# Regrouping an expert's whole-array products, splitting one weight unit elsewhere, and holding one GpSimd product

## The chip, the cores and the metric

The kernel runs on 1 core of one Trainium2 chip. The metric is the device time of one execution in microseconds (us), as the median of the runs. The engines are TensorE (PE), VectorE (DVE), ScalarE (ACT), GpSimd (POOL) and SyncE (SP), whose queue starts the weight transfers.

## What is computed

An activation of 256 x 1024 passes two blocks in float32. The first has a mixer (stick-breaking attention beside a gated recurrence) and a mixture of 16 experts; the second has an ffn, a sparse-attention mixer and another ffn. Cut to what the change touches:

```python
def hgrn2_chunk_scan(q, k, log_f, v):          # gated recurrence, 8 heads of 64
    ...
        scores = jnp.einsum('bhtk,bhsk,bhtsk->bhts', qc, kc, decay)
        o = (jnp.einsum('bhts,bhsv->bhtv', scores, vc)
             + jnp.einsum('bhtk,bhkv->bhtv', qc * jnp.exp(cum), state))
...
def hier_moe(h, w_rg, b_rg, w_re, b_re, w_gate, w_up, w_down):
    ...
    for e in range(N_EXPERTS):                 # 16 experts, D_EXPERT = 512
        a = jax.nn.silu(t @ w_gate[e]) * (t @ w_up[e])
        y = y + combine[:, e:e + 1] * (a @ w_down[e]).astype(f32)
...
def swiglu(h, w_in, w_out):                    # both ffns, D_FF = 2816
    ...
    return (jax.nn.silu(gate) * up) @ w_out
```

Each token goes to two experts of one group of four, so the kernel gathers the tokens of an expert into 64 columns, works on these, and scatters the results back with a product.

## The kernel before, in words

The stages follow each other, and their spans in the profiled execution are: first mixer 0 to 236 us, experts (`moe`) 236 to 450, first `ffn` to 650, second mixer (`mixer2`) to 766, last `ffn` to the end. All weights pass once through SBUF: `Stream.load` puts units of 1 MB on SP's queue (L107), each into a slot that the users of an earlier unit gave back. The order in which a weight unit is posted is thus tied to the work that frees its slot.

Most weights are split into a high part, copied by ScalarE (L353 in `split_next`), and a low part, a subtraction by VectorE (L365, function `low`; its engine can be given). Three products are then summed: high by high, high by low, low by high. `split_next` posts the next load behind the low part. `unit` takes a split unit, splits the next one, and runs what stands in `pend`.

**Recurrence** (`hgrn`, L835 to 958) is one of the generators whose steps are laid between the projections of the first mixer. It goes through levels; in each, VectorE and GpSimd make scaled copies of keys and queries (L875, L883, L886, L888), TensorE multiplies them, and VectorE merges the scores (L900). The last level has the product of L903 instead. Afterwards two products `o = ih * dg` on GpSimd (L926) need nothing from the levels; VectorE adds TensorE's result `hpo` to each (L928). In this stage a scheduler of the language orders most of the work.

**Experts** (`moe`, from L963) are in an order written by hand. The loop at L1248 does for expert e: the first half of gate and up of expert e + 1 (`gate_up(e + 1, 0)`, L1193: 16 products, which use the array as 128*64), then `act(e)` (four transposes of the stored gate/up results into `pst`, L1205; silu on ScalarE, L318; the product `at` on VectorE, L1208) and `spread(e)` (two products `pso` from one-hot rows, L1215; VectorE takes from them `sc`, L1217, and `ws`, L1219). Then comes `gate_up(e + 1, 1)`, which ends with two ScalarE copies of the accumulated bank `gu` to `gs` (L1199); `scatter(e - 1)` (four whole-array products into `Y`, L1246); in three of the experts `gather` for the next group (L1129); and `down(e)` (16 products `dn`, 128*64, L1231, evacuated by ScalarE at L1238 and VectorE at L1240). `gu`, `pst`, `pso` and `dn` take turns in four PSUM banks.

**First ffn** (`ffn`, L1417): for each of 22 hidden tiles q, VectorE takes the sums from PSUM to `sg` (L1450). The function `later`, run within the next unit, has the silu (ScalarE), the product with the second half (VectorE, L1454) and the split into `ah` and `al` (L386, L387). Output units follow for pairs of tiles (L473 to L490). After the last one, `then` adds PSUM to `x` (L1486), multiplies by the norm gain to `y` (L1490), and TensorE transposes `y` (L1379) for the second mixer, whose first product is L1607. The weights of that first product are split after output unit NFT//2 - 2, with the low part on GpSimd.

Of the kernel before, what the change touches and what calls it, by code (L numbers as in the profile page):

```python
# [10 lines left out]
F32 = mybir.dt.float32  # L11
# [4 lines left out]
OP = mybir.AluOpType  # L16
# [6 lines left out]
NFT = FF // 128  # L23
E = 16
# [244 lines left out]
class K:  # L269
# [565 lines left out]
    def hgrn(self):  # L835
        nc, P = self.nc, self.P
        t4 = lambda n, **k: P.tile([128, 4, 256], F32, name=n, tag="t4", bufs=T4)
        sg, qh = self.sgf, self.qh
# [30 lines left out]
        for l in range(8):  # L869
            h = 1 << l  # L870
            nb = 256 // (2 * h)
            v = lambda x: x.rearrange("p f (b w i) -> p (f b) w i", w=2, i=h)
            if h > 1:
                self.act(1, v(kz)[:, :, 0], v(suf)[:, :, 0], AF.Exp)
                nc.vector.tensor_tensor(out=v(kz)[:, :, 0], in0=v(kz)[:, :, 0], in1=v(kk)[:, :, 0], op=OP.mult)  # L875
            else:
                nc.vector.tensor_copy(v(kz)[:, :, 0], v(kk)[:, :, 0])
            self.act(1, v(kz)[:, :, 1], v(pre)[:, :, 1], AF.Exp)
            if l < 7:
                w = lambda x: x.rearrange("p f (t b w i) -> p (f t) b w i", t=2, w=2, i=h)[:, :, :, 1]  # L880
                for g in range(2):
                    r = slice(g * 64, g * 64 + 64)
                    nc.vector.tensor_tensor(out=qq[r, :, g].rearrange("p a (b i) -> p a b i", i=h),  # L883
                                            in0=w(kz)[r], in1=w(qh)[r], op=OP.mult)
                B = [128, 4 * nb, h]
                nc.gpsimd.tensor_tensor(out=v(suf)[:, :, 0], in0=v(suf)[:, :, 0],  # L886
                                        in1=v(pre)[:, :, 1, h - 1:h].to_broadcast(B), op=OP.add)
                nc.gpsimd.tensor_tensor(out=v(pre)[:, :, 1], in0=v(pre)[:, :, 1],  # L888
                                        in1=v(pre)[:, :, 0, h - 1:h].to_broadcast(B), op=OP.add)
                yield 0, W_HG  # L890
                pss = [self.ps.tile([128, 4, 2, 64], F32, name=f"hs{t}", tag="s") for t in range(2)]
                for t in range(2):
                    for f in range(4):
                        nc.tensor.matmul(pss[t][:, f].rearrange("p g c -> p (g c)"), kz[:, f, t * 128:t * 128 + 128],
                                         qq[:, 2 * f + t].rearrange("p g c -> p (g c)"), start=True, stop=True)
                yield 1750, 0
                mk = self.c1[:, A_HM + l * 64:A_HM + l * 64 + 64].bitcast(I32).rearrange("p (b i) -> p b i", i=h)
                for t in range(2):
                    ac = acc[:, :, t].rearrange("p a (b w i) -> p a b w i", w=2, i=h)[:, :, :, 1]
                    nc.vector.copy_predicated(ac, mk[:, None].to_broadcast([128, 8, 64 // h, h]),  # L900
                                              pss[t].rearrange("p f g (b i) -> p (f g) b i", i=h))
            else:
                nc.vector.tensor_tensor(out=v(kz)[:, :, 1], in0=v(kz)[:, :, 1], in1=v(qh)[:, :, 1], op=OP.mult)  # L903
                yield 0, W_HG

                pss = [self.ps.tile([128, 4, 128], F32, name=f"hs{g}", tag="s") for g in range(2)]
                for f in range(4):
                    for g in range(2):
                        r = slice(g * 64, g * 64 + 64)
                        nc.tensor.matmul(pss[g][:, f], kz[r, f, :128], kz[r, f, 128:], start=True, stop=True)  # L910
                yield 1750, 0
                cross = t4("cross").rearrange("p a (b c) -> p (a b) c", b=2)
                for g in range(2):
                    nc.scalar.copy(cross.rearrange("p (f g) c -> p f g c", g=2)[:, :, g], pss[g])
            yield 0, 300
# [4 lines left out]
        for t in range(2):  # L920
            po = self.ps.tile([128, 8, 64], F32, name="hpo", tag="s")
            for hd in range(8):
                if t == 1:
                    nc.tensor.matmul(po[:, hd], cross[:, hd], ih[:, 0, hd], start=True, stop=False)
                nc.tensor.matmul(po[:, hd], acc[:, hd, t], ih[:, t, hd], start=t == 0, stop=True)
            nc.gpsimd.tensor_tensor(out=o[:, t], in0=ih[:, t],  # L926
                                    in1=dg[:, t, :, None].to_broadcast([128, 8, 64]), op=OP.mult)
            nc.vector.tensor_tensor(out=o[:, t], in0=po, in1=o[:, t], op=OP.add)  # L928
            yield 1700 * (1 + t), 300
        self.st.add(P, "b8", 3, U_FFN1 - 8)  # L930
# [32 lines left out]
    def moe(self, x, po):  # L963
# [3 lines left out]
        with tc.manual_schedule():  # L967
# [216 lines left out]
            def gate_up(e, u):  # L1184
                c = slice((e % 4) * CAP, (e % 4) * CAP + CAP)
                if u == 0:
                    GU[e] = PS.tile([128, 512], F32, name="gu", tag="d")
                rw = [self.st.pop() for _ in range(2)]
                for k in range(4):
                    kk = 4 * u + k  # L1190
                    for i in range(2):
                        w = _part(rw[i][0], k, 4, 512)
                        nc.tensor.matmul(GU[e][i * 64:i * 64 + 64], XT[u][:, k, c], w, start=kk == 0, stop=kk == 7)  # L1193
                for _, sl in rw:
                    self.st.load(sl)
                if u:
                    g, GS[e] = GU.pop(e), [P.tile([128, 256], F32, name="gs", tag="sba", bufs=2) for _ in range(2)]
                    for h in range(2):
                        nc.scalar.copy(GS[e][h], g[:, h * 256:h * 256 + 256])  # L1199

            def act(e):
                ps = PS.tile([128, 4, 128], F32, name="pst", tag="d")
                gs = GS.pop(e)
                for f in range(4):
                    nc.tensor.transpose(ps[:, f], gs[f // 2][:, f % 2 * 128:f % 2 * 128 + 128], self.ident)  # L1205
                at = AT[e] = P.tile([128, 4, CAP], F32, name="at", tag="sbs", bufs=2)
                self.act(4, at, ps[:, :, :CAP], AF.Silu)
                V.tensor_tensor(out=at, in0=ps[:, :, CAP:], in1=at, op=OP.mult)  # L1208
# [39 lines left out]
            for e in range(-1, E):  # L1248
                if e == 2:
                    most = nc.values_load(cnti[0:1, 0:1], min_val=0, max_val=S)  # L1250
                if e == 13:
                    two = self.g12()
                    next(two)
                if e + 1 < E:
                    gate_up(e + 1, 0)
                if 0 <= e < E - 1:
                    act(e)
                    spread(e)
                    if e % 4 == 3:
                        doubled(e // 4 + 1)  # L1260
                if e + 1 < E:
                    gate_up(e + 1, 1)
                if e % 4 == 0 and e < 12:
                    onehot(e // 4 + 1)
                if e == E - 1:
                    down(e)
                if e >= 1:
                    scatter(e - 1)
                if e % 4 == 2 and e < E - 2:
                    for j in range(4):  # L1270
                        for i in range(2):
                            gather(e // 4 + 1, j, i)
                if e == E - 2:
                    next(two)
                    act(E - 1)
                    spread(E - 1)
                if 0 <= e < E - 1:
                    down(e)
# [138 lines left out]
    def ffn(self, x, Y=None, last=False):  # L1417
# [5 lines left out]
        with ExitStack() as ctx:  # L1423
# [24 lines left out]
            def ev(q, ps):  # L1448
                sg, ah, al = w[0].rearrange("p (a b) c -> p a b c", a=2)[:, q % 2], w[1][:, q % 4], w[2][:, q % 4]
                V.tensor_tensor(out=sg, in0=ps, in1=rb[:, None].to_broadcast([128, 2, 256]), op=OP.mult)  # L1450

                def later():
                    self.act(ep, sg[:, 0], sg[:, 0], AF.Silu)
                    V.tensor_tensor(out=sg[:, 0], in0=sg[:, 1], in1=sg[:, 0], op=OP.mult)  # L1454
                    self.split(ah, al, sg[:, 0])
                    A[q] = (ah, al)

                self.pend.append(later)

            po = None  # L1460
            for kind, i in FFN_ORDER:
# [30 lines left out]
                        los.append(self.turn(y, 0, c.start // 512, xh, "s"))  # L1492

                self.out_unit(po, lambda k: A[k], 2 * i, i == 0, ends, then=then)
                if i == NFT // 2 - 2 and not last:
                    self.split_next(True)(nc.gpsimd)
            if not last:
                for h in range(2):
                    los.append(self.turn(y, 1, h, xh, "s"))
# [730 lines left out]
```

## Time and profile before

| | us |
|---|---|
| median of 3 runs | 960.9 (960.53 to 961.39) |
| the profiled execution | 961.63 |
| its span | 959.9 |
| PE busy in the span | 935.5 (97%) |
| DVE busy | 540.3 (56%) |
| ACT busy | 406.9 (42%) |
| POOL busy | 107.3 (11%) |

A timeline row has the start, the length from the first start to the last end of a run of like instructions, the engine, the line, the operation, output and inputs by name, tile shape, form and count; in brackets stands the idle time of the engine before it and what ended it. Lengths of neighbouring PE rows overlap, since a matmul begins before the last has drained; what a group costs the sequence is the distance between starts.

### The profile page before, as it was taken

The numbers are of one execution on the slowest core, as the hardware profiler recorded it, in microseconds if no ns is written. First come the engines' busy times: TensorE is split into PE (matmuls) and PEld (weight loads), VectorE is DVE, ScalarE is ACT, GpSimd is POOL, SyncE is SP. The second block draws the span as 40 slices with busy tenths as digits, with TensorE's granted clock in tenths as the row PEclk, the third lists the DMA queues.
The fourth block names the chain that finished last, engine by engine and source line by source line (L and its number), as shares of the span: only waits on it lengthen the run. The fifth ranks groups of instructions, "written<-read, shape, count | busy, mean of one in ns | idle before, by whom it ended". The sixth has DMA issues, their size and how long they took to land.

```text
span 959.9 us, 15041 instructions
## 1 busy us (share of the span) xinstructions
PE 935.5 (97%) x6192; PEld 747.3 (78%) x6192; DVE 540.3 (56%) x849; ACT 406.9 (42%) x640; POOL 107.3 (11%) x114
## 2 busy tenths in 40 slices
PE   6999999999999999997999999999999999999998
PEld 5997899996343433433999999988977899999997
DVE  5589848666222121213765655576888665655555
ACT  5445654443121111213644434436748643434432
POOL 4153304032000000023200000020000000000000
PEclk9999999999999999999999999999999999999999
DMA  8743365688999999996555555637351355555511
GB/s 341 276 158 131 101 247 179 245 327 349 383 420 418 418 418 417 421 415 249 188 192 189 189 175 182 204 120 280 128 217 48 107 188 189 176 181 183 195 56 44
DMA packets 39031, 224.30 MB, mean 234 GB/s; under 512 B 4372, under 2 KB 7221, under 8 KB 16816
## 3 DMA queue, kind: packets, MB, share of 16 engines
q1 hardware_dynamic: 38224, 221.57, 61.9%
q0 software_dynamic: 592, 1.61, 0.5%
q8 instruction: 50, 0.82, 0.4%
q14 instruction: 21, 0.17, 0.0%
q10 hardware_dynamic: 144, 0.13, 0.0%
HBM read 222.22 MB, written 1.07 MB: 233 GB/s over the span
## 4 chain that ended last, share of the span: by engine, by line
PE 50%; DVE 1%; ACT 1%; issue 1%; POOL 0%; POOLq 0%
PE psa L419 8%; PE psa L415 8%; PE psa L414 8%; PE po L483 8%; PE po L490 4%; PE po L1607 2%; PE p L1607 2%; PE qa L1607 1%; PE qb L1607 1%; PE pt L1789 1%; PE psa L404 1%; PE po L473 1%; PE sc L1770 1%; PE pa L1607 1%; DVE y L1490 1%
## 5 line engine op out<-in xcount | busy, mean ns | idle before, releaser
L365 DVE TENSOR_TENSOR wlo<-raw,whi 128x2048 fp32r<-128x2048 f32 (+2 forms) x98 | 214.2, 2190 | 54.4 <-ACT whi L353 53.3
L353 ACT ACTIVATE whi<-raw 128x2048 fp32r<-128x2048 f32 (+2 forms) x100 | 180.5, 1808 | 139.6 <-issue 98.0
L414 PE MATMUL psa<-hTh,whi 128*128 128x256 f32 x928 | 228.3, 283 | 0.0
L415 PE MATMUL psa<-hTl,whi 128*128 128x256 f32 x928 | 227.9, 283 | 0.0
L415 PEld LDWEIGHTS psa<-hTl,whi 128*128 128x128 f32 x928 | 177.9, 192 | 0.5 <-issue 0.2
L414 PEld LDWEIGHTS psa<-hTh,whi 128*128 128x128 f32 x928 | 177.9, 192 | 0.3
L419 PE MATMUL psa<-hTh,wlo 128*128 128x256 f32 x928 | 130.4, 283 | 0.0
L419 PEld LDWEIGHTS psa<-hTh,wlo 128*128 128x128 f32 x928 | 119.7, 192 | 0.3 <-issue 0.2
L1193 PE MATMUL gu<-raw,XT 128*64 128x512 f32 x512 | 115.8, 595 | 0.0
L1193 PEld LDWEIGHTS gu<-raw,XT 128*64 128x64 f32 x512 | 35.3, 137 | 66.2 <-issue 62.5
L1240 DVE SCALAR_TENSOR_TENSOR ds<-dn,ws,ds 64x512 fp32r<-64x512 f32 x32 | 24.0, 749 | 110.1 <-ACT ds L1238 109.6
L1450 DVE TENSOR_TENSOR sg<-psa,rb 128x512 f32<-128x512 f32 x44 | 30.3, 692 | 81.2 <-PE psa L419 77.6
L386 ACT ACTIVATE ah<-sg 128x256 fp32r<-128x256 f32 x44 | 18.4, 418 | 104.4 <-DVE sg L1454 104.4
L1231 PE MATMUL dn<-raw,at 128*64 128x512 f32 x256 | 58.2, 598 | 0.0
L483 PE MATMUL po<-whi,ah 128*128 128x512 f32 (+1 forms) x180 | 50.1, 368 | 0.0
L483 PE MATMUL po<-whi,al 128*128 128x512 f32 (+1 forms) x180 | 49.8, 366 | 0.0
L1238 ACT ACTIVATE ds<-dn,ws 64x512 fp32r<-64x512 f32 x32 | 21.8, 683 | 60.0 <-PE dn L1231 59.8
L1231 PEld LDWEIGHTS dn<-raw,at 128*64 128x64 f32 x256 | 17.1, 136 | 32.7 <-issue 29.5
L490 PE MATMUL po<-wlo,ah 128*128 128x512 f32 (+1 forms) x180 | 40.2, 367 | 0.0
L483 PEld LDWEIGHTS po<-whi,al 128*128 128x128 f32 x180 | 32.4, 188 | 6.1
L490 PEld LDWEIGHTS po<-wlo,ah 128*128 128x128 f32 x180 | 31.7, 188 | 5.9
L1592 DVE TENSOR_TENSOR wlo<-raw,whi 128x1024 fp32r<-128x1024 f32 (+2 forms) x28 | 31.6, 1151 | 8.3 <-ACT whi L1588 8.3
(486 smaller groups left out, 1345.3 us busy)
## 6 DMA issues: line engine op xcount, KB each, us to landing
raw<-W SPq DMA_DIRECT2D x173, 1024.0 KB, 5.5
raw<-W SPq DMA_DIRECT2D x60, 512.0 KB, 11.8
bt<-dr SPq DMA_DIRECT2D x2, 1024.0 KB, 9.2
raw<-W SPq DMA_DIRECT2D x2, 816.0 KB, 4.5
raw<-W SPq DMA_DIRECT2D x2, 768.0 KB, 4.2
gain<-gains POOLq DMA_DIRECT2D x2, 512.0 KB, 7.7
out<-x SPq DMA_DIRECT2D x3, 256.0 KB, 2.0
x<-x SPq DMA_DIRECT2D x2, 256.0 KB, 3.7
```

Of the source, the lines that this page charges most:

```text
L353: i = self.nc.scalar.activation(hi[:, o], r, AF.Copy).ins
L365: i = eng.tensor_tensor(out=lo[:, o], in0=r, in1=hi[:, o].bitcast(F32), op=OP.subtract).ins
L414: nc.tensor.matmul(ps[:, c % 2], hi[:, k, cs], xh[:, k, :], start=k == 0, stop=False)
L415: nc.tensor.matmul(ps[:, c % 2], hi[:, k, cs], xl[:, k, :], start=False, stop=False)
L419: nc.tensor.matmul(ps[:, c % 2], lo[:, k, cs], xh[:, k, :], start=False, stop=k == kt - 1)
L483: nc.tensor.matmul(p, x[:, ts], hi[:, k, c], start=first and k == 0 and x is xh, stop=False)
L490: nc.tensor.matmul(p, xh[:, ts], lo[:, k, c], start=False, stop=False)
L1193: nc.tensor.matmul(GU[e][i * 64:i * 64 + 64], XT[u][:, k, c], w, start=kk == 0, stop=kk == 7)
L1231: nc.tensor.matmul(ps[h % len(ps)][R[h]], AT[e][:, f], _part(raw, k, 2, 1024)[:, h * 512:h * 512 + 512], start=f == 0, stop=f == 3)
L1450: V.tensor_tensor(out=sg, in0=ps, in1=rb[:, None].to_broadcast([128, 2, 256]), op=OP.mult)
L1592: i = V.tensor_tensor(out=two[u][1][:, s], in0=unit(u)[0][0][:, s], in1=two[u][0][:, s].bitcast(F32), op=OP.subtract)
L1607: i = nc.tensor.matmul(out(), l, r, start=first and n == 0, stop=last, skip_group_check=True)
```

## The change

In `hgrn`, a dependency makes the two GpSimd products of L926 wait for VectorE's last-level product (L903). In `moe`, for e from 1 to 14, both halves of gate and up of expert e + 1 come first, then the transposes and silu of expert e, then the two `gs` copies (now a function `keep`), then `pso`, the scatter products of e - 1 and the down products of e; for e = 0 the order stays. In the first `ffn`, the split of the second mixer's first unit moves into `later` of the last hidden tile: the high part follows the silu on ScalarE, and the low part, now on VectorE, follows the split of that tile.

```diff
--- before.py
+++ after.py
@@ -900,7 +900,7 @@
                     nc.vector.copy_predicated(ac, mk[:, None].to_broadcast([128, 8, 64 // h, h]),
                                               pss[t].rearrange("p f g (b i) -> p (f g) b i", i=h))
             else:
-                nc.vector.tensor_tensor(out=v(kz)[:, :, 1], in0=v(kz)[:, :, 1], in1=v(qh)[:, :, 1], op=OP.mult)
+                end = nc.vector.tensor_tensor(out=v(kz)[:, :, 1], in0=v(kz)[:, :, 1], in1=v(qh)[:, :, 1], op=OP.mult).ins
                 yield 0, W_HG
 
                 pss = [self.ps.tile([128, 4, 128], F32, name=f"hs{g}", tag="s") for g in range(2)]
@@ -923,8 +923,10 @@
                 if t == 1:
                     nc.tensor.matmul(po[:, hd], cross[:, hd], ih[:, 0, hd], start=True, stop=False)
                 nc.tensor.matmul(po[:, hd], acc[:, hd, t], ih[:, t, hd], start=t == 0, stop=True)
-            nc.gpsimd.tensor_tensor(out=o[:, t], in0=ih[:, t],
-                                    in1=dg[:, t, :, None].to_broadcast([128, 8, 64]), op=OP.mult)
+            i = nc.gpsimd.tensor_tensor(out=o[:, t], in0=ih[:, t],
+                                        in1=dg[:, t, :, None].to_broadcast([128, 8, 64]), op=OP.mult).ins
+            self.tc.add_manual_dep(i, end.name, mybir.DependencyInfo(
+                mybir.DependencyClass.Sync, mybir.DependencyReason.DATA), reason="the port is shared")
             nc.vector.tensor_tensor(out=o[:, t], in0=po, in1=o[:, t], op=OP.add)
             yield 1700 * (1 + t), 300
         self.st.add(P, "b8", 3, U_FFN1 - 8)
@@ -1193,10 +1195,11 @@
                         nc.tensor.matmul(GU[e][i * 64:i * 64 + 64], XT[u][:, k, c], w, start=kk == 0, stop=kk == 7)
                 for _, sl in rw:
                     self.st.load(sl)
-                if u:
-                    g, GS[e] = GU.pop(e), [P.tile([128, 256], F32, name="gs", tag="sba", bufs=2) for _ in range(2)]
-                    for h in range(2):
-                        nc.scalar.copy(GS[e][h], g[:, h * 256:h * 256 + 256])
+
+            def keep(e):
+                g, GS[e] = GU.pop(e), [P.tile([128, 256], F32, name="gs", tag="sba", bufs=2) for _ in range(2)]
+                for h in range(2):
+                    nc.scalar.copy(GS[e][h], g[:, h * 256:h * 256 + 256])
 
             def act(e):
                 ps = PS.tile([128, 4, 128], F32, name="pst", tag="d")
@@ -1251,15 +1254,23 @@
                 if e == 13:
                     two = self.g12()
                     next(two)
+
+
                 if e + 1 < E:
                     gate_up(e + 1, 0)
-                if 0 <= e < E - 1:
+                if e == 0:
                     act(e)
+                    spread(e)
+                if e + 1 < E:
+                    gate_up(e + 1, 1)
+                if 0 < e < E - 1:
+                    act(e)
+                if e + 1 < E:
+                    keep(e + 1)
+                if 0 < e < E - 1:
                     spread(e)
                     if e % 4 == 3:
                         doubled(e // 4 + 1)
-                if e + 1 < E:
-                    gate_up(e + 1, 1)
                 if e % 4 == 0 and e < 12:
                     onehot(e // 4 + 1)
                 if e == E - 1:
@@ -1451,9 +1462,12 @@
 
                 def later():
                     self.act(ep, sg[:, 0], sg[:, 0], AF.Silu)
+                    low = self.split_next(True) if q == NFT - 1 and not last else None
                     V.tensor_tensor(out=sg[:, 0], in0=sg[:, 1], in1=sg[:, 0], op=OP.mult)
                     self.split(ah, al, sg[:, 0])
                     A[q] = (ah, al)
+                    if low:
+                        low()
 
                 self.pend.append(later)
 
@@ -1492,8 +1506,6 @@
                         los.append(self.turn(y, 0, c.start // 512, xh, "s"))
 
                 self.out_unit(po, lambda k: A[k], 2 * i, i == 0, ends, then=then)
-                if i == NFT // 2 - 2 and not last:
-                    self.split_next(True)(nc.gpsimd)
             if not last:
                 for h in range(2):
                     los.append(self.turn(y, 1, h, xh, "s"))
```

## Rows read from the trace of the kernel before

**Rows 1.** Busy time by stretch: us, each engine (count), PE clock, DMA share, GB/s
```profile
110.00:117.00 7.00, 7.00 (x43) 5.92 (x40) 6.83 (x10) 4.63 (x11) 5.92 (x5) 1.00 0.46 152
...
236.00:449.80 213.80, 212.82 (x1035) 85.66 (x1033) 50.62 (x126) 47.02 (x94) 15.21 (x20) 1.00 0.98 399
```

**Rows 2.** Timeline of PE, one expert: start, length, line, tiles, count
```profile
349.21 3.60 PE L1193 MATMUL gu<-raw,XT 128*64 128x512 f32 x16
352.74 0.66 PE L1205 MATMUL pst<-cst,gs 128*128 128x128 f32 x4
353.24 0.32 PE L1215 MATMUL pso<-icb,ob 128*128 128x176 bf16 x2
353.48 3.65 PE L1193 MATMUL gu<-raw,XT 128*64 128x512 f32 x16
357.06 1.20 PE L1246 MATMUL Y<-ds,sc 128*128 128x512 f32 x4
358.19 3.65 PE L1231 MATMUL dn<-raw,at 128*64 128x512 f32 x16
```

**Rows 3.** Timeline of PE where the experts begin
```profile
236.23 10.52 PE L1193 MATMUL gu<-raw,XT 128*64 128x512 f32 x48
246.69 0.66 PE L1205 MATMUL pst<-cst,gs 128*128 128x128 f32 x4
```

**Rows 4.** Timeline of PE near the last experts
```profile
432.08 1.51 PE L1193 MATMUL gu<-raw,XT 128*64 128x512 f32 x6
...
436.70 1.08 PE L1308 MATMUL pg<-gparts 128*128 128x512 f32 x4
```

**Rows 5.** Timeline of ACT and DVE in the expert of rows 2
```profile
357.26 0.65 ACT L1199 COPY gs<-gu 128x256 f32<-128x256 f32 x2 [3.44 <-PE gu L1193]
...
353.85 0.42 DVE L1208 TENSOR_TENSOR at<-pst,at 128x256 f32<-128x256 f32 x1 [1.48 <-ACT at L318]
```

**Rows 6.** Waits of PE's weight loads, 240:460: total us, times, longest
```profile
PEld dn L1231 <- ACT gs L1199: 1.8, 5, 0.4
```

**Rows 7.** Loads issued from L107 in 409.3:413, with their time to landing
```profile
L107 SPq DMA_DIRECT2D raw<-W x2: 327/328/328, 409.5 to 412.0; - x2
...
DMA to landing us min/median/max: 10.2/10.8/11.4
```

**Rows 8.** Timeline of PE at the end of the first ffn
```profile
645.86 0.66 PE L1379 MATMUL pst<-cst,y 128*128 128x128 f32 x4 [1.62 <-DVE y L1490]
...
649.84 0.66 PE L1379 MATMUL pst<-cst,y 128*128 128x128 f32 x4 [0.67 <-DVE y L1490]
```

**Rows 9.** Timeline of DVE at the same place
```profile
635.71 2.29 DVE L365 TENSOR_TENSOR wlo<-raw,whi 128x2048 fp32r<-128x2048 f32 x1 [0.30 <-ACT whi L353]
...
641.55 0.69 DVE L1486 SCALAR_TENSOR_TENSOR x<-po,x 128x512 f32<-128x512 f32 x1 [2.30 <-PE po L473]
642.28 3.52 DVE L1490 TENSOR_TENSOR y<-x,gain 128x512 f32<-128x512 f32 x1
...
646.44 0.69 DVE L1490 TENSOR_TENSOR y<-x,gain 128x512 f32<-128x512 f32 x1
```

**Rows 10.** Timeline of POOL at the same place
```profile
640.67 4.58 POOL L365 TENSOR_TENSOR wlo<-raw,whi 128x2048 fp32r<-128x2048 f32 x1 [171.85 <-ACT whi L353]
...
646.64 0.59 POOL L1555 TENSOR_SCALAR qsc<-vec 128x2 f32<-128x2 f32 x1
```

**Rows 11.** Timeline of ACT at the same place
```profile
638.37 0.42 ACT L386 ACTIVATE ah<-sg 128x256 fp32r<-128x256 f32 x1 [2.39 <-DVE sg L1454]
638.70 1.90 ACT L353 ACTIVATE whi<-raw 128x2048 fp32r<-128x2048 f32 x1
```

**Rows 12.** Timeline of POOL in the first mixer
```profile
113.16 2.95 POOL L926 TENSOR_TENSOR ho<-ih,dg 128x512 f32<-128x512 f32 x2
```

**Rows 13.** Timeline of DVE in the first mixer
```profile
112.20 3.00 DVE L883 TENSOR_TENSOR qz<-kz,qh 64x512 f32<-64x512 f32 x2
...
127.83 0.56 DVE L790 SCALAR_TENSOR_TENSOR sbt<-z,sbt 128x384 f32<-128x384 f32 x1 [4.12 <-ACT sbt L318]
```

## The prediction, written before the change was run

> **What bounds the kernel now.** I read the busy time by stretches first. In the experts' stretch TensorE is busy 212.82 of 213.80 us at the full granted clock, and VectorE, the next of the others, 50.62 [rows 1]. A change there can win only by shortening TensorE's own sequence, or lose by opening a gap in it. TensorE's timeline of one expert shows that sequence, and the distance from start to start is what each group really costs: half of gate/up 3.53, transposes 0.50, the `pso` products 0.24, the other half 3.58, scatter products `Y` 1.13, then `dn` [rows 2]. Shapes alternate: `gu` and `dn` use the array as 128*64, `pst`, `pso` and `Y` as 128*128, so an expert switches four times. The timeline of the tail of the first ffn then shows the one place where TensorE stands still for another engine near this change: 1.62 us for `y`, and 0.67 for the last `y` [rows 8]. VectorE's and GpSimd's rows of the same moment say why (below).
>
> **Experts, e from 1 to 14.** The old order is half, pst, pso, half, Y, dn; the new one is half, half, pst, pso, Y, dn: two switches instead of four. Nothing is removed from the work; gaps between groups are. (a) At the start of the stage three halves run in a row, 236.23 to 246.69, which is 10.46 or 3.49 each [rows 3]. Two halves then take 6.97, where the split ones take 3.53 + 3.58 = 7.11 [rows 2]: 0.14 saved. (b) `Y` after tiled work takes 1.20 for four products [rows 2]; four products of the same shape that follow whole-array work take 1.08 [rows 4]: 0.12 saved. (c) The step from `pso` back to tiled work sits in pso's 0.24. In the new order `Y` follows; between 0 and 0.12 goes, and I take 0.06, the middle, since no row shows pso followed by `Y`. Sum 0.32.
>
> What could fill the gap again is the chain that `dn` waits for. From the start of pst to the end of VectorE's product `at` it takes 353.85 + 0.42 - 352.74 = 1.53 [rows 2, 5]. Before, 3.58 of tiled products and `Y` lay over it. Now only the rest of pst, pso and `Y` do: 0.50 + 0.18 + 1.01 = 1.69. That leaves 0.16 of cover, so the wait moves to the edge without appearing. The two copies `gs` of the next expert (0.65) now run on ScalarE behind that silu. The silu ends when VectorE's product starts, 353.85, so they end 353.85 + 0.65 - 352.74 = 1.76 after the start of pst [rows 2, 5]. Whoever is queued behind them on ScalarE (the evacuation of `dn`) needs nothing so early, and the transposes that read them come some 12 us later. They count only where `dn` is placed in the PSUM bank that these copies free, which happened to five experts before [rows 6]; there `dn` would start at 1.76 instead of 1.69, 0.07 late. So I take 0.30 for each expert: 14 x 0.30 = 4.2. The bounds are 2.1 (0.15 each: the halves alone) and 5.3 (0.38 each: all of pso's step too). Expert 0 keeps its order.
>
> The weights come from SP's queue at 399 GB/s with the DMA engines 0.98 busy in this stage [rows 1], so TensorE takes weights faster than they come and draws down a lead. The closest unit I found is expert 15's second half: its last load was issued at 412.0, landed 10.2 later at 422.2 and is used from 432.08 [rows 4, 7], 9.9 ahead. Taking 4.2 off leaves over 5, so the stream isn't late. I cost it at nothing; when that lead is gone, the whole 4.2 goes.
>
> **First split of the second mixer.** Removed: GpSimd's 4.58 us subtraction at 640.67 to 645.25 [rows 10]. VectorE's `y` product, which reads two SBUF operands, started at 642.28 in the middle of it and took 3.52; the same product at 646.44 took 0.69 [rows 9]. The `x` operation at 641.55, also inside that interval and with one operand in PSUM, kept its 0.69 [rows 9]. So `y` was held for 2.8, and TensorE waited 1.62 for it [rows 8].
>
> Added: ScalarE's hi copy (1.90) directly behind the silu of the last activation. ScalarE was idle 2.39 there, so `ah` at 638.37 isn't moved [rows 11]. VectorE's lo product follows `al`; the like product on VectorE takes 2.29, and VectorE was idle 2.30 before `x` at 641.55 [rows 9]. It fits with nothing to spare. The unit's next weight load on SP, queued behind lo, leaves earlier than before; nothing waits for that. With `y` at about 0.69 it ends at 642.97 instead of 645.80, before TensorE's output products end (it waited until 645.86 for 1.62, so they end at 644.24) [rows 8]. The wait of 1.62 goes. What is late next: the last `y` still follows the last `x` and TensorE's last products, and TensorE waited 0.67 for it at 649.84 [rows 8]. VectorE, no longer 2.83 behind, comes to it earlier by more than TensorE does; of the 0.67 I let 0.6 go, by re-laying the two engines' rows with `y` at 0.69. 1.62 + 0.6 = 2.2. Bounds: 1.62 (that wait alone) and 2.83 (the whole stretch of `y`).
>
> [...]
>
> **The held product in the first mixer.** The two products of L926 ran 113.16 to 116.11 [rows 12] and two VectorE products beside them took 3.00 together [rows 13] where 0.69 is normal for one of that kind [rows 9]: 1.6 held. But TensorE was busy 7.00 of 7.00 in that stretch [rows 1], and VectorE stood idle 4.12 later, before 127.83, waiting for ScalarE [rows 13]. The product moves behind the last level, into that idle time. The waiting product holds back, on GpSimd's queue, only the DMA of `hgn` at L932; its own reader L928 comes behind TensorE's products into `hpo`, which follow the last level in any case. A gain could reach 0.8 (half of what was held, if the scan's later products come earlier) and a loss 1.5 (one product of L926 held in front of a VectorE one). I take 0, for the full TensorE.
>
> **Sum.** 4.2 + 2.2 + 0 = 6.4 off. The profiled execution took 961.63, so its successor takes 955.2. It lay 0.7 above the median of the runs, 960.9, so the median goes to 954.5.
>
> **Rivals.** B: the chain pst, silu, `at` takes longer than its 0.16 of cover, by 0.3 or so, and `dn` waits where the switches were. For it: the cover is thin and crosses three engines. Against: all its durations are from rows. Experts save nothing; 960.9 - 2.2 = 958.7.
>
> C, slower: the order of releases puts `pso` of expert e into the bank of `gu` of e + 1. Before, those copies came after `pso`, so it couldn't be; now `gu` is complete before the transposes, but its copies come behind the silu. `pso` then starts at 1.76 instead of 0.50, 1.26 late, and `Y` and `dn` behind it. Each such expert loses 1.26 - 0.30 = 0.96. All 14: 13.4 - 2.2 = 11.2 slower, 972.1. It decides from six experts on (6 x 1.26 = 7.6 against 6.4). For it: `dn` did meet such a bank five times [rows 6]. Against: the tags and their order of use are unchanged and `pso` has four banks to take from.
>
> D: the weights' lead is gone before expert 15; 958.7 as in B. Against: 9.9 of lead [rows 4, 7].
>
> E: small GpSimd operations that read SBUF, like `qsc` with 0.59 [rows 10], begin ahead of a `y` and block it. If each of the last two is held for that long, 2 x 0.59 = 1.2 is lost: 955.7, and up to 957 if the zero spare of lo is overrun too. Against: the `y` at 646.44 ran at 0.69 beside `qsc`, having begun first [rows 9, 10].
>
> F: the change does nothing measurable: both gains turn into other waits; 960.9.
>
> **How the numbers follow.** Forecast A, 954.5, has 0.70 with its own range 953 to 956.5. B 0.09, C 0.07, D 0.04, E 0.06, F 0.04. The low end takes the upper bounds together: 960.9 - 5.3 - 2.8 - 0.8 = 952.0. The high end takes in B and D with 0.5 for the first mixer: 959.2; C and F are left out. About 0.2%, 1.9 us, can be told from no change, so faster means under 959.0. A, E and 0.07 of B and D lie there: 0.83. The rest of B and D with F: 0.10. C: 0.07.
>
> **What would show it.** In the profile after: the group of `gu` with 32 products in 6.97, then pst, pso, `Y` with 1.08, and `dn` without a wait for `at`, at a period 0.3 shorter; a wait of `dn` on L1208 of about 0.3 is B, of `pso` on the copies is C, of `gu` on a DMA is D. In the tail `y` at 0.69 and no wait of 1.62; a `y` above 1 with a small GpSimd operation beside it is E. In the first mixer the two products at 0.69 and the products of L926 after the last level, with later TensorE work where it was. The prediction is wrong if the period doesn't fall, or if the first stage's end moves by over 1 us.

## The result and the profile after

The changed kernel takes 954.16 us (953.13 to 954.41) against 960.89; the ratio is 0.9928, interval 0.9910 to 0.9945. Timed twice more (after_again and after_third below) it took 953.45 and 954.14, the ratio 0.9926 both times. One of the six executions of the last timing took 3236.8 us, for a reason that nothing here shows, and is left out. The forecast was 954.5, range 952.0 to 959.2. So 6.7 to 7.2 us are gone where 6.4 were forecast; the profiled executions differ by 7.5, 961.63 to 954.1.

Where they went is read from TensorE's timeline of both traces, at the starts of the same groups:

| group on TensorE | before | after | later or earlier | in this stretch |
|---|---|---|---|---|
| 29th product of the run | 15.84 | 15.48 | -0.36 | -0.36 |
| first `gu` of the experts | 236.23 | 235.29 | -0.94 | -0.58 |
| `Y` of expert 13 | 435.67 | 430.46 | -5.21 | -4.27 |
| first psa of the ffn | 456.68 | 450.58 | -6.10 | -0.89 |
| first qb of the second mixer | 650.25 | 642.32 | -7.93 | -1.83 |

The first row is scatter of the start: in the traces of all 14 executions that product comes between 14.76 and 16.46. The experts gave the 4.2 that was forecast. The stretch behind them gave 0.9 that no step of the prediction has, of which the next stretch takes some back, and the first mixer gave a little too. (psa are the sums of the ffn's first products, qb those of the second mixer's.)

The experts' timeline of TensorE after the change (start, length, line, tiles, count), for rows 2:

```profile
346.13 7.04 PE L1195 MATMUL gu<-raw,XT 128*64 128x512 f32 x32
353.10 0.66 PE L1208 MATMUL pst<-cst,gs 128*128 128x128 f32 x4
353.59 0.32 PE L1218 MATMUL pso<-icb,ob 128*128 128x176 bf16 x2
353.70 1.17 PE L1249 MATMUL Y<-ds,sc 128*128 128x512 f32 x4
354.80 3.65 PE L1234 MATMUL dn<-raw,at 128*64 128x512 f32 x16
358.28 7.04 PE L1195 MATMUL gu<-raw,XT 128*64 128x512 f32 x32
```

The period is 358.28 - 346.13 = 12.15, where rows 2 give 12.46 (their five steps and 3.48 from `dn` to the next `gu`). The two halves take 353.10 - 346.13 = 6.97, `pst` 0.49, `pso` 0.11, `Y` 1.10. No bracket stands behind `dn`: TensorE doesn't wait. ScalarE and VectorE in the same expert, for rows 5:

```profile
353.79 0.39 ACT L318 ACTIVATE at<-pst 128x256 f32<-128x256 f32 x1 [6.07 <-PE pst L1208]
354.07 0.64 ACT L1202 COPY gs<-gu 128x256 f32<-128x256 f32 x2
...
354.21 0.42 DVE L1211 TENSOR_TENSOR at<-pst,at 128x256 f32<-128x256 f32 x1 [4.92 <-ACT at L318]
```

`at` ends at 354.63, 1.53 after `pst` began, and `dn` starts at 1.70. The end of the first ffn, for rows 8, 9 and 11, in the timelines of VectorE, ScalarE and TensorE:

```profile
632.24 0.42 DVE L1466 TENSOR_TENSOR sg<-sg 128x256 f32<-128x256 f32 x1
...
633.48 2.29 DVE L365 TENSOR_TENSOR wlo<-raw,whi 128x2048 fp32r<-128x2048 f32 x1
635.87 0.69 DVE L1500 SCALAR_TENSOR_TENSOR x<-po,x 128x512 f32<-128x512 f32 x1
636.60 0.69 DVE L1504 TENSOR_TENSOR y<-x,gain 128x512 f32<-128x512 f32 x1
...
630.21 1.91 ACT L353 ACTIVATE whi<-raw 128x2048 fp32r<-128x2048 f32 x1
...
640.23 1.04 PE L1390 MATMUL pst<-cst,y 128*128 128x128 f32 x8
641.90 0.66 PE L1390 MATMUL pst<-cst,y 128*128 128x128 f32 x4 [0.64 <-DVE y L1504]
642.32 1.17 PE L1619 MATMUL qb<-whi,hTh 128*128 128x512 f32 x4
```

`y` takes 0.69, the low part lies in VectorE's gap without moving `x`, and of TensorE's waits the last, 0.64, is left. From the last tile's product (L1454 before at 637.92, L1466 here) to the first `qb` it was 650.25 - 637.92 = 12.33 and is 10.08: 2.25 less.

### The profile page after: what moved, and what is told of

Read it like the earlier page. It is cut to its first block, busy times and chain, and to the rows that moved or that the text cites. A ratio compares the mean times of both kernels' runs of the same rounds, so it can differ in the third digit from the quotient of the medians.

```text
span 952.0 us, 15016 instructions
## 1 busy us (share of the span) xinstructions
PE 931.3 (98%) x6192; PEld 749.1 (79%) x6192; DVE 538.8 (57%) x850; ACT 405.3 (43%) x640; POOL 101.0 (11%) x113
## 4 chain that ended last, share of the span: by engine, by line
PE 51%; ACT 1%; issue 1%; DVE 1%; POOL 0%; POOLq 0%; DVEq 0%
PE psa L419 8%; PE psa L415 8%; PE psa L414 8%; PE po L483 8%; PE po L490 4%; PE po L1619 2%; PE p L1619 2%; PE qa L1619 1%; PE po L473 1%; PE qb L1619 1%; PE pt L1801 1%; PE psa L404 1%; PE sc L1782 1%; PE pa L1619 1%; PE pst L1390 0%
## 5 line engine op out<-in xcount | busy, mean ns | idle before, releaser
L365 DVE TENSOR_TENSOR wlo<-raw,whi 128x2048 fp32r<-128x2048 f32 (+2 forms) x99 | 216.6, 2192 | 53.9 <-ACT whi L353 52.8
L1195 PE MATMUL gu<-raw,XT 128*64 128x512 f32 x512 | 112.7, 592 | 0.0
L1211 DVE TENSOR_TENSOR at<-pst,at 128x256 f32<-128x256 f32 x16 | 6.8, 425 | 76.0 <-ACT at L318 76.0
L318 ACT ACTIVATE at<-pst 128x256 f32<-128x256 f32 x16 | 6.2, 386 | 88.4 <-PE pst L1208 88.3
```

The lines of the kernel that those rows point to most:

```text
L365: i = eng.tensor_tensor(out=lo[:, o], in0=r, in1=hi[:, o].bitcast(F32), op=OP.subtract).ins
```

## Experiments

**Each part alone, and the whole again.** The three kernels are the kernel before with one part of the diff each: the new loop of `moe`, the moved `split_next`, the dependency in `hgrn`.

> The kernel before with the experts' new order alone. Theory (switches of the array's shape): fourteen experts of 12.15 instead of 12.46, so 4.3 us less between the first gate/up product and the scatter products of expert 13; in all about 956.6. In the changed kernel's trace the stretch after the experts (to the first psa product of the ffn) was also 0.9 shorter. Rival 1: that gain belongs to the new order too, then the total is nearer to 955.8. Rival 2 (the wait for the activation takes the place of the switches): a period of 12.4 or more and a total within 1 us of before.

956.63 against 960.68, ratio 0.9956 (0.9943 to 0.9970): 4.05 less.

> The kernel before with the moved first split of the second mixer alone, low part on VectorE. Theory (GpSimd's 4.6 us subtraction held VectorE's y): y takes 0.69 instead of 3.52, TensorE's wait of 1.62 goes, and the mixer's first product comes 2.1 us earlier against the products before it; total about 958.8. Rival (the experts' gain only showed here, by another phase of the weight stream): the tail keeps its wait, total 960.9.

958.09 against 960.68, ratio 0.9973 (0.9962 to 0.9984): 2.6 less. In its trace the first `qb` comes at 647.45 with the tail's only wait 0.64, as in the whole change.

> The kernel before with the two held GpSimd products alone. The record said 0, with bounds of 0.8 less and 1.5 more. Theory from the two traces: VectorE's two qz products take 2.25 instead of 3.00, the work behind them comes 0.8 to 1.3 earlier, and TensorE no longer waits twice 0.19 for ScalarE's sba at the values' products; 0.4 less, total 960.5. Rival (the first stage's 0.9 in the trace is the scatter of the start alone): the values' products stand where they stood, shift constant from the first 20 us on, total 960.9.

959.48 against 960.68, ratio 0.9991 (0.9982 to 1.0000): at the edge of what a timing can tell. Its trace has 1.1 from the start's scatter, and 0.4 more at the place that is told below.

> The changed kernel once more, on the chip of the single parts. Theory (the parts add up): the sum of the three parts' differences within 0.5 us, 954.2 in all. Rival (the parts share a gain, or the stretch after the experts is a matter of chance): the sum misses by over 0.5, and the stretch from the last transposes of the experts to the first psa product differs from the 6.7 of the first trace.

953.45 against 960.68, 7.2 less. The parts sum to 4.05 + 2.6 + 1.2 = 7.85; the miss of 0.6 is over the 0.5 that was set, but inside the intervals of the three; hold_only's timing gives 0.8 more than its trace does. That the parts share nothing isn't shown closer than that.

**How much cover the experts' chain has.** Two copies lengthen it:

```diff
+                for _ in range(2 if 0 < e < E - 1 else 0):
+                    nc.scalar.copy(at, ps[:, :, :CAP])
                 self.act(4, at, ps[:, :, :CAP], AF.Silu)
```

> The changed kernel with two extra ScalarE copies of pst ahead of the silu, for e from 1 to 14: work that is not needed, to lengthen the chain that dn waits for by 0.66 (two of 0.38, 0.33 apart). Theory (the chain of 1.53 has 0.17 of cover under pst, pso and Y, 1.70 together): dn starts 2.19 after the transposes, 0.49 late in each expert, TensorE shows that wait for VectorE's at, and the kernel takes 6.9 more than the changed one, about 960.7. Rival (the wait is hidden, since weight loads and products already queued run ahead): under 2 more, below 956.

961.18 against 961.17 (ratio 0.9999, 0.9989 to 1.0008): 7.0 to 7.7 more than the changed kernel, all of the change's gain. TensorE and VectorE in one expert of it:

```profile
344.86 0.66 PE L1208 MATMUL pst<-cst,gs 128*128 128x128 f32 x4
...
347.25 0.65 PE L1236 MATMUL dn<-raw,at 128*64 128x512 f32 x2 [0.62 <-DVE at L1213]
...
346.78 0.42 DVE L1213 TENSOR_TENSOR at<-pst,at 128x256 f32<-128x256 f32 x1 [5.73 <-ACT at L318]
```

`dn` starts 2.39 after `pst`, 0.69 later than in the changed kernel. The copies added 0.40 each to the silu's start and not 0.33: `at` ends at 347.20, 2.34 after `pst`, against 1.53. `dn` follows 0.05 behind it. So the whole chain is 1.53 + 0.05 = 1.58 in the changed kernel, under 1.70 of cover: 0.12 is free, and all beyond goes to TensorE one for one (0.81 - 0.12 = 0.69).

That holds for five of the experts. TensorE's waits in this trace (us in all, times, longest) name a second chain:

```profile
PE dn L1236 <- ACT gs L1202: 3.5, 5, 0.7
PE dn L1236 <- DVE at L1213: 3.1, 5, 0.6
```

In five others `dn` waits for the `gs` copies, which stand behind the silu on ScalarE and free the PSUM bank that `dn` takes. They end 2.43 after `pst` and `dn` starts at 2.48, 0.78 late. In the changed kernel they end at 1.62, so this chain is 1.62 + 0.05 = 1.67, and only 0.03 of its cover is free. The three experts with gather products between `Y` and `dn` aren't late. Five times 0.69 and five times 0.78 are 7.4; up to `Y` of expert 13 the trace has 7.3. The expectation counted fourteen times 0.49: its 6.9 came near by luck. That the loss equals the change's gain is chance too.

The same wait where the change left the old order, in expert 0:

```diff
-                if e == 0:
-                    act(e)
-                    spread(e)
                 if e + 1 < E:
                     gate_up(e + 1, 1)
-                if 0 < e < E - 1:
+                if 0 <= e < E - 1:
                     act(e)
```

(and the same bound for its `spread`)

> The changed kernel with expert 0 in the new order too, where no scatter products stand between pso and dn. Theory (dn waits for the chain through the silu, 1.53 and 0.05 for the signal, which there has only pst and pso, 0.74, over it): TensorE shows a wait of 0.8 to 0.9 for VectorE's at ahead of the first dn, the halves give 0.14 back, so 0.7 more in that expert. Rival (nothing waits, since products queue ahead): 0.14 to 0.3 less in that expert. In the total neither is over 0.1%; the trace decides.

```profile
235.38 13.95 PE L1195 MATMUL gu<-raw,XT 128*64 128x512 f32 x64
249.27 0.65 PE L1208 MATMUL pst<-cst,gs 128*128 128x128 f32 x4
...
250.85 3.65 PE L1234 MATMUL dn<-raw,at 128*64 128x512 f32 x16 [0.78 <-DVE at L1211]
```

TensorE waits 0.78 for `at`, again 1.58 behind `pst`; from the first `gu` to `dn` it takes 15.47 where the changed kernel takes 14.68. In total 954.47, as expected not to be told from 954.14 beside it. The order of the halves pays only where `Y` stands behind them.

**Which step of the switching costs what.** `spread(e)` is moved behind `scatter(e - 1)`:

> The changed kernel with the scatter products of e - 1 between the transposes and the pso products of e, for e from 1 to 14. In the changed kernel pso takes 0.11 and Y 1.10 from start to start, 1.21 together; before it was 0.24 and 1.13. Theory (a step between whole-array and 128*64 work costs the same whoever takes it): pso, now last, takes 0.24 again and Y about 1.0, sum 1.24, so 0.03 an expert more, total within 0.5 of the changed kernel's 953.5 to 954.2. Rival (Y's first pair is slow because the bfloat16 products of pso stand ahead of it): Y takes 0.92 or less, 1.3 us gained over the stage, total about 952.5.

```profile
353.23 0.66 PE L1208 MATMUL pst<-cst,gs 128*128 128x128 f32 x4
353.65 1.17 PE L1249 MATMUL Y<-ds,sc 128*128 128x512 f32 x4
354.66 0.33 PE L1218 MATMUL pso<-icb,ob 128*128 128x176 bf16 x2
354.92 3.65 PE L1234 MATMUL dn<-raw,at 128*64 128x512 f32 x16
```

`pst` 0.42, `Y` 1.01, `pso` 0.26: 1.69, where the change has 0.49 + 0.11 + 1.10 = 1.70. Whoever stands last pays the step back to 128*64 work: `Y` 1.10 against 1.01, `pso` 0.26 against 0.11. The rival falls: `Y` has its slow first pair (1.17 in length) behind the transposes too. The kernel took 952.7 (ratio 0.9903, 0.9888 to 0.9919), 0.8 to 1.5 less than the changed kernel's three timings, outside the 0.5 that was expected and near the rival's 952.5. The intervals overlap, and the experts' rows, 0.01 apart, don't explain a difference; it is left open.

**Engine or place of the low part.** First the new place, but GpSimd (`low(nc.gpsimd)` in `later`):

> The changed kernel with the moved split's low part on GpSimd again, at the new place. Theory (a GpSimd operation that reads two SBUF operands holds a VectorE operation that does so too): the 4.6 us now lie on the last tile's product and on al, which take some 3 to 4 instead of 0.42; al comes about 3 late for TensorE's last output products, y stays at 0.69; 2.9 to 3.6 more than the changed kernel, about 957. Rival (what helped is that the split begins earlier, whichever engine has the low part): as the changed kernel, 953.5 to 954.2.

958.28 against 961.17 (0.9967, 0.9955 to 0.9978), 4.1 to 4.8 more than the changed kernel; 2.9 to 3.6 were expected. VectorE's, GpSimd's and TensorE's rows, and then a stretch with TensorE's clock (the number behind POOL's):

```profile
632.12 4.79 DVE L1466 TENSOR_TENSOR sg<-sg 128x256 f32<-128x256 f32 x1
...
632.07 4.56 POOL L365 TENSOR_TENSOR wlo<-raw,whi 128x2048 fp32r<-128x2048 f32 x1 [168.32 <-ACT whi L353]
...
637.41 0.64 PE L473 MATMUL po<-whi,ah 128*128 128x512 f32 x1 [2.38 <-ACT ah L386]
...
637.40:641.00 3.60, 3.59 (x8) 2.66 (x9) 1.79 (x3) 0.00 (x0) 0.89 (x6) 0.53 0.84 285
```

The product of two SBUF operands that takes 0.42 in the changed kernel takes 4.79: it began 0.05 after GpSimd's and ends 0.3 behind its end. TensorE waits 2.38 and then runs its products 0.43 apart instead of 0.23: 0.2 after the wait had ended the granted clock fell to 0.50, where it stayed until 641.0 (0.53 is the mean of the stretch, which begins before the fall). That second loss was not expected. Then the old place, but VectorE (`self.split_next()` behind the output unit, in the kernel before):

> The kernel before with the split of the second mixer's first unit at its old place, behind the output unit, and only the low part moved from GpSimd to VectorE. Theory: the high part still ends at 640.60, low takes VectorE from 640.6 to 642.9, x starts 1.35 later than before but y takes 0.69 and ends at 644.3; TensorE's wait of 1.62 falls to about 0.1 and the last transposes come 1.4 earlier; total about 959.3, so the engine gives 1.4 and the place 0.7 to 1.1 more. Rival (VectorE's 2.3 takes the place of the 2.8 that y was held): within 0.5 of before, 960.5.

959.88 against 961.17 (0.9983, 0.9974 to 0.9992), 1.3 less. In its trace `x` starts at 642.50 behind the low part, `y` takes 0.69, and from L1454 to `qb` it is 648.37 - 637.59 = 10.78. So of the tail's 2.25 in the traces the engine gives 1.55, the place 0.7.

**The stretch behind the experts.** It gave 0.9, unforeseen. Before and after, TensorE's timeline there:

```profile
449.13 0.63 PE L1379 MATMUL pst<-cst,y 128*128 128x128 f32 x4 [0.36 <-DVE y L1438]
454.23 2.79 PE L1379 MATMUL pst<-cst,y 128*128 128x128 f32 x12 [4.47 <-issue]
```

```profile
443.90 1.12 PE L1390 MATMUL pst<-cst,y 128*128 128x128 f32 x7 [0.36 <-DVE y L1449]
448.85 2.08 PE L1390 MATMUL pst<-cst,y 128*128 128x128 f32 x9 [3.84 <-issue]
```

TensorE stops in the middle of 16 transposes, with no semaphore to wait for. Counting TensorE's instructions in the traces from 0, weight loads and semaphore instructions among them, gives the place:

| kernel | branch over `moe_rest` is number | instructions from it to the stop | transposes before the stop |
|---|---|---|---|
| before, and each kernel with the old order of the experts | 5396 | 14 | 4 |
| after, three times, and the three others with its expert loop | 5388 | 22 | 7 |
| scatter_first | 5379 | 31 | 12 |
| first_expert_too | 5387 | 23 | 8 |

The sum is 5410 every time, though the instruction behind the stop is a product in some kernels and a weight load or a semaphore instruction in others. The experts' new order needs eight semaphore instructions fewer on TensorE. The stop begins at a fixed place of the program and ends 5.8 to 6.5 after the jump; more of the transposes then come ahead of it, 0.11 apart at a granted clock of 1.00, and fewer behind it, 0.21 apart at 0.50. From the first transposes to psa it is 7.5 to 7.8 in the four traces with the old order and 5.7 to 6.9 in the eight with the new one that the table has.

The DMA packets show what comes in just before the stop ends. The profile names the packets of queue q8 `instruction`: 50 of them, of 16 KB each, one for every 252 to 256 of TensorE's instructions (medians of the traces). The changed kernel's packets in 446:448 have one of them (packets, MB, share of 16 engines):

```profile
q8 instruction: 1, 0.02, 2.9%
```

It starts at 446.62, 3.8 after the jump (442.80), and lands at 447.56; TensorE goes on at 448.85. In each of the 14 traces exactly one such packet lies between the jump and the end of the stop. It starts 3.5 to 4.5 after the jump and takes 0.9 to 1.0, and TensorE goes on 1.3 to 1.6 after it has landed. That the stop is a wait for this packet is an estimate from these times alone; that the jump starts its transfer, and what fills the time before it, isn't shown.

Two kernels test what the place is worth. One makes four `pso` products twice, which puts the branch back to number 5396:

> The changed kernel with four of the pso products made twice (experts 2 and 4), eight more TensorE instructions, which puts the branch over moe_rest where the kernel before had it in TensorE's program. Theory (the stretch behind the experts became shorter because the experts' new order needs eight instructions fewer, so that seven transposes and not four come ahead of the stop): four transposes ahead of the stop, and 7.5 instead of 6.0 to 6.9 from the first transposes to the first psa product; 0.7 more than the changed kernel and 0.2 for the doubled products, about 954.6. Rival (the order itself does it): seven ahead of the stop, as in the changed kernel, 953.7 to 954.4.

```profile
444.81 0.63 PE L1391 MATMUL pst<-cst,y 128*128 128x128 f32 x4 [0.36 <-DVE y L1450]
449.62 2.79 PE L1391 MATMUL pst<-cst,y 128*128 128x128 f32 x12 [4.18 <-issue]
452.06 3.67 PE L404 MATMUL psa<-hTh,whi 128*128 128x256 f32 x16
```

Four transposes again, with the experts in the new order, and 7.25 from the first transposes to psa where the changed kernel has 6.68 to 6.86. 954.61 in total, beside this one:

> The changed kernel beside the other three on one chip: 953.5 to 954.2.

954.14. The 0.5 between the two totals is inside their scatter; the four transposes decide. The other test makes the jump come earlier:

```diff
-            scatter(E - 1)
             self.in_order = False
         with tc.If(most > CAP):
             self.moe_rest(Y, U)
+        with tc.manual_schedule():
+            self.in_order = True
+            scatter(E - 1)
+            self.in_order = False
```

> The changed kernel with the last expert's scatter products moved behind the branch over moe_rest. In the traces so far TensorE jumps over that branch, runs 14 to 31 more instructions, always up to the same place of its program, and stands still until 6.0 to 6.3 after the jump; then it runs at half clock. Theory (the jump starts the fetch of what follows that place): the jump comes about 2.3 earlier, TensorE goes on 2.3 earlier, the still time falls from 3.8 to about 1.5; 2.3 less than the changed kernel, and up to 2.4 more if the clock no longer falls: 949 to 951.5. Rival (the still time is something that the ffn's first transposes wait for, not the jump): TensorE goes on where it did, 953.5 to 954.2.

949.4 against 960.9, ratio 0.9877 (0.9863 to 0.9892), 4.7 less than the changed kernel beside it: faster than either kernel of this study.

```profile
440.94 1.20 PE L1249 MATMUL Y<-ds,sc 128*128 128x512 f32 x4
443.50 1.16 PE L1249 MATMUL Y<-ds,sc 128*128 128x512 f32 x4 [1.36 <-DVEq L1291]
444.90 1.05 PE L1393 MATMUL pst<-cst,y 128*128 128x128 f32 x7 [0.24 <-DVE y L1452]
447.63 1.14 PE L1393 MATMUL pst<-cst,y 128*128 128x128 f32 x9 [1.69 <-issue]
448.59 2.19 PE L404 MATMUL psa<-hTh,whi 128*128 128x256 f32 x16
...
448.60:450.60 2.00, 2.00 (x18) 2.00 (x17) 1.86 (x3) 2.00 (x3) 1.10 (x2) 1.00 0.47 78
```

The jump is at 440.8 and TensorE goes on at 447.63, 6.8 later; the stop, again behind number 5410, is 1.69 long, since the last four `Y` products now come behind the jump and fill part of the time. From the first of the two `Y` groups TensorE goes on 1.9 earlier than in after_third and reaches psa 2.7 earlier, so the rival falls. The clock stays at 1.00, and the first psa group takes 450.62 - 448.59 = 2.03, where the changed kernel needs 454.14 - 450.58 = 3.56 for it. 2.7 and 1.5 are most of the 4.7.

## Why the prediction came out right, and which steps didn't

**Experts: the term held, its parts didn't.** 4.2 was forecast, 4.27 is in the trace, 4.05 in the timing of the part alone. The halves gave the 0.14. The other two were read wrongly, by about as much each way: `pso`'s step back was put at 0.06 and gave 0.13 (0.24 to 0.11); `Y`'s entry was put at 0.12 and gave 0.03 (1.13 to 1.10). The 1.08 of [rows 4] was the length of products that follow `Y` itself, of the same kind; scatter_first shows that `Y` begins slowly behind whole-array work also. 0.14 + 0.13 + 0.03 + 0.01 (`pst`) = 0.31.

**Cover.** 1.69 against a chain of 1.53 was forecast, 1.70 against 1.58 is what the runs show: the signal from `at` to TensorE was left out of the chain. Rival B was thus 0.12 away and not 0.16. For the five experts whose `dn` takes the bank that the `gs` copies free, the prediction put the copies' end at 1.76 and `dn` 0.07 late. They end at 1.62, and `dn` starts at 1.70 to 1.71 in every expert where `Y` stands right ahead of it: none is late, by 0.03. Rival C didn't occur: `pso` follows the transposes at once. D neither: in the changed kernel no product of the experts waits for a transfer on TensorE.

**Tail.** 2.2 forecast, 2.25 in the trace, 2.6 alone. The wait of 1.62 went whole. Of the last wait, 0.67, the prediction let 0.6 go; 0.64 is left. What came in its place is a pause that it had not looked at: the transposes of the second and third `y` started at 647.74 and 648.51 before, and stand in one row of eight now, 0.41 apart, which is 0.36 less; the rest comes in steps under 0.2. Rival E rested on GpSimd's small operations coming out near the `y`s. They weren't near: with nothing in front of them on GpSimd's queue they ran early in the ffn, in the changed kernel at

```profile
463.91 0.26 POOL L1567 TENSOR_SCALAR qsc<-vec 128x2 f32<-128x2 f32 x1
...
640.22 0.20 POOL L1878 MEMSET hs<- 128x128 f32 x1 [175.84 <-PE po L473]
```

The first is `qsc`; GpSimd's next operation after this group comes when it has stood idle for 175.84. The prediction asked which y they would meet, and not when the queue would let them go. What a small GpSimd operation does to a `y` that begins after it, no run shows. The hold by GpSimd's subtraction is there again in low_gpsimd_early: 4.79 for a VectorE operation of 0.42, beside the subtraction's 4.56.

**First mixer: a term at 0 that is 0.4.** The step that failed is "TensorE is busy 7.00 of 7.00 in that stretch". It was, but the delay reached it later. VectorE's `qz` pair takes 2.25 now (3.00 before, [rows 13]); the work behind it, ScalarE's too, moves up 0.8, and TensorE's weight loads of the values' products no longer wait for ScalarE. Before, and after:

```profile
120.85 0.19 PEld L415 LDWEIGHTS psa<-hTl,whi 128*128 128x128 f32 x1
121.23 0.19 PEld L811 LDWEIGHTS ot<-sba,vs 128*64 128x64 f32 x2 [0.19 <-ACT sba L318]
121.61 0.13 PEld L811 LDWEIGHTS ot<-sba,vs 128*64 128x64 f32 x1 [0.19 <-ACT sba L318]
...
122.41 0.19 PEld L419 LDWEIGHTS psa<-hTh,wlo 128*128 128x128 f32 x1 [0.17 <-issue]
```

```profile
120.34 0.19 PEld L415 LDWEIGHTS psa<-hTl,whi 128*128 128x128 f32 x1
120.67 0.20 PEld L811 LDWEIGHTS ot<-sba,vs 128*64 128x64 f32 x4
...
121.47 0.19 PEld L419 LDWEIGHTS psa<-hTh,wlo 128*128 128x128 f32 x1 [0.17 <-issue]
```

1.56 between the same two loads became 1.13: 0.43. From the 29th product to the experts' first `gu` it is 219.8 to 220.0 in the ten traces with the held products and 220.4 in the four without. A row of busy time hides such a wait, and the right reading was to follow VectorE's delay to the next thing that TensorE took from ScalarE. 0.43 lies inside the bound that was given for a gain.

The 1.6 that the prediction put down to the products of L926 was half of that. GpSimd and VectorE in the changed kernel:

```profile
111.27 1.39 POOL L888 TENSOR_TENSOR pre<-pre 128x512 f32<-128x512 f32 x1
111.66 2.25 DVE L883 TENSOR_TENSOR qz<-kz,qh 64x512 f32<-64x512 f32 x2
```

The first product of the pair takes 1.54 before and after, beside GpSimd's operation of L888, which the change doesn't move. Only the second was held by a product of L926, and fell from 1.45 to 0.69. The forecast that both would take 0.69 failed.

**What the sum left out.** The stretch behind the experts wasn't in it. It gave 0.9 up to psa in the profiled pair, and varies: from the last four scatter products to a product well inside the ffn (TensorE's products 2656 and 2801 of the run) it is 25.0 to 26.0 in the four traces with the old order, 24.0 to 25.6 in eight with the new (eight_more and branch_earlier apart), because the clock's return varies: TensorE runs at half clock for 2.6 to 6.0 behind the stop. The means are 0.8 apart. So 0.4 and some 0.8 were not forecast, more than the excess over 6.4 in the three timings (0.3, 0.8, 0.4). The forecast was right in its two large terms, and a little luckier than its working.

## What to carry to other kernels

Gather work by the shape in which it uses the array, but weigh the saving per switch (0.15 here, 0.31 for two) against the cover that the old order gave to chains across engines: 0.12 was left over one and 0.03 over the other, and beyond that a delay came through in full (0.81 - 0.12 = 0.69). An operation is costed at nothing only when its delay has been followed to the next wait of the bounding engine, however far behind. Where an engine stands still with nothing to wait for, count its instructions up to the stop in two builds: the same number in both (5410 here) points at the program, and not at the data, and the packets of q8 can then be laid beside the stop.

## What the runs showed of the hardware

In this kernel TensorE stands still at a fixed instruction (number 5410 in all 14 traces), 14 to 34 instructions behind the jump over code that isn't run and not at it, and goes on 5.8 to 6.8 after the jump. The stop ends 1.3 to 1.6 after a packet of 16 KB has landed on q8, which moves 0.82 MB in 50 such packets, one for every 252 to 256 of TensorE's instructions. The packet itself takes 0.9 to 1.0; that some 6 us pass from the jump to the end of the stop is shown only beside this kernel's weight stream.

Behind the longer stops the granted clock was lower too. After 3.4 to 4.8 of standing still TensorE's granted clock was 0.50 for 2.6 to 6.0 us of the work behind it, and after a wait of 2.38 it was 0.50 for 3.4; after the stop of 1.69 it stayed at 1.00.
